# Two transformer blocks on one core: the recurrence's input products in another order, its far decays by biased exponentials, and the queries' norm sums in one piece

## The chip, the cores and the metric

One core of a Trainium2 chip runs the whole program, one launch. The time is device microseconds from the first to the last instruction of that core, with what lies around it; lower is better. The engines are PE (TensorE, matrix products), DVE (VectorE), ACT (ScalarE), POOL (GpSimd) and SP (SyncE, which issues the loads). Each runs its own list of instructions in order and waits at semaphores for the others.

## What is computed

Two blocks, one after the other, on x of 512 tokens by 1024 features, all in float32. The first block is a gated mixer and a feed-forward layer; its mixer has a gMLP branch and a recurrence over 8 heads of width 128:

```python
log_f = jax.nn.log_sigmoid(zf32)            # forget gate
k = jax.nn.sigmoid(-zf32)
q = jax.nn.silu(zq.astype(jnp.float32))
# per chunk of 64 tokens, cum = cumsum(log_f):
o_inter = einsum('bhtk,bhkv->bhtv', qb * exp(cum), state)
scores  = einsum('bhtk,bhsk,bhtsk->bhts', qb, kb, decay)   # decay = exp(cum_t - cum_s), s <= t
state   = state * exp(last) + einsum('bhsk,bhsv->bhkv', kb * exp(last - cum), vb)
# over all chunks, then:
o = rmsnorm(o, norm_g) * jax.nn.silu(heads(zo))
```

The second block is a short convolution mixer with a feed-forward layer, then attention over 16 heads of width 64 with forget gates, whose queries and keys are normalized per head (`rmsnorm_2(q, q_norm)`), and a second feed-forward layer.

## The kernel before, in words

Activations lie with features on the partitions (128 by 512 tokens per tile). Every product is made of three float32r products of high and low halves: `mm3` (L200 to L203) issues xh by wh, xl by wh and xh by wl into one PSUM tile, each 128x512. A product over 1024 inputs (`mm_T`, L205) is eight such triples, and yields after each; `mm_N` (L231) is its form with the tokens on the partitions, four PSUM tiles side by side, 32 yields. Weights are loaded in 1 MB pieces in the order of the list `plan`, and split into halves by ACT (`wh`, L180) and DVE (`wl`, L181), two products ahead of use.

The recurrence of the first block is not run token by token. For each head, `head_in` makes the products zf, zq and zo, and from zf the running sums `sc[:, 1]` (`cum`, sums of log f inside each chunk of 64) and `sc[:, 0]`, the keys `kq[:, 0]` and queries `kq[:, 1]`. `Core.decays(n)` then makes, for level n of 0 to 8, a tile `dec` with the keys and queries scaled for pairs of tokens whose blocks of 2^n tokens are neighbours: for n below 6 POOL subtracts the middle sum twice, and ACT takes the exponential; for n of 6 to 8 the sums are changed in place by DVE (at 7 and 8 two additions of 128x256 each) before one exponential of 128x512. A product by the queries on DVE (POOL at levels 1 and 3) ends each level. `small`, `mid` and `far` are the PE products of levels 0 to 4, 5 to 6 and 7 to 8, all into tiles named `lv`; `values` multiplies by the values (`o`), `square` and `norm` make the sum of squares of the output (`oss`) and its inverse root, and `done` the gated output `y`.

Two generators are woven by `weave`: `main` with the big products of the heads, `side` with the steps of `Core`; `side` starts after HGSTART yields of `main`, and then advances in proportion HGW. A head's `Core` can start only when `head_in` has put it into `heads`; decays of the next head are made up to AHEAD = 4 levels early. `v` is made by `zi_half`, one `mm_N` for four heads each. PE's order follows the weave; the order on ACT, DVE and POOL is set when the program is built, by a scheduler that places what is ready, except for instructions that are pinned (`pin`) to the order of the program.

In the attention stage `HeadNorm` reads a product of queries or keys (`hn`, DVE), squares it (ACT or POOL), splits the square into `hsh` (ACT) and `hsl` (DVE or POOL), sums both over 64 partitions by two products with `bones` on PE (`sums`), and goes on with `hm` (DVE) and `hr` (ACT). `start_norms` issues `sums` for a query after seven of the eight triples of the next product.

Of the kernel before, what the change touches and what calls it, by code (L numbers as in the profile page):

```python
# [8 lines left out]
F32 = mybir.dt.float32  # L9
# [4 lines left out]
ALU = mybir.AluOpType  # L14
# [22 lines left out]
N_FILL = 3  # L37
AHEAD = 4
N_DEC = 8
HGSTART = 36  # L40
HGW = (130, 60)
MUL_POOL = (1, 3)

# [13 lines left out]
def tile_two_blocks(ctx: ExitStack, tc: tile.TileContext, a: dict, out: bass.AP):  # L57
# [137 lines left out]
    def ahead(n):  # L195
        for j in range(state["prep"], n):
            prep(j)
            state["prep"] = j + 1

    def mm3(ps, lh, ll, rh, rl, start, stop_):  # L200
        pe.matmul(ps, lhsT=lh, rhs=rh, start=start, stop=False)  # L201
        pe.matmul(ps, lhsT=lh, rhs=rl, start=False, stop=False)  # L202
        pe.matmul(ps, lhsT=ll, rhs=rh, start=False, stop=stop_)  # L203

# [88 lines left out]
    zf = plan_T("zf", w_in, 0, KD, 2048, 1024)  # L293
    zq = plan_T("zq", w_in, 0, KD, 1024, 1024)
    zo = plan_T("zo", w_in, 0, KD, 4096, 1024)
    for h in range(8):
        if h % 4 == 0:
            plan += plan_N("zi", w_in, 0, KD, 3072 + h * 128)
        plan += [zf[h], zq[h], zo[h]]
    ga = plan_T("ga", w_in, 0, KD, 5120, 1024)  # L300
    ua = plan_T("ua", a["w_up_a"][0], 0, 4, 0, 1024, 512)
    for i in range(8):
# [304 lines left out]
    pool.memset(reset, 1.0)  # L607
    pool.memset(pieces(reset, 64)[:, :, 0:1], 0.0)
    hgs = cp.tile([128, 1], F32, name="hgs")
    ts(dve, hgs, V("hg"), -0.5, ALU.mult)  # L610
    v = [[None, None] for _ in range(NT)]

    def view2(t2, h):
# [4 lines left out]
        return t.rearrange("p (b j i) -> p b j i", j=2, i=h)  # L618

    Y = []  # L620
    heads = {}

    def silu(p, o, g=None):
        t = T("z")
# [15 lines left out]
    def head_in(h):  # L640
        kq, sc = T2("kq"), T2("sc")
        p = yield from mm_T("zf", X)
        t = T("zf")
        tt(dve, t, p, rb)
        e = T("e")
        stt(e, t, -1.0, t, ALU.mult, ALU.min)
        f(e, e, AF.Exp)
        f(e, e, AF.Ln, bias=1.0)
        g = T("g")
        stt(g, t, 0.0, e, ALU.min, ALU.subtract)  # L650
        dve.tensor_tensor_scan(out=sc[:, 1, :], data0=reset, data1=g, initial=0.0, op0=ALU.mult, op1=ALU.add)  # L651
        stt(e, t, 0.0, e, ALU.max, ALU.add)

        tt(pool, sc[:, 0, :], sc[:, 1, :], e, ALU.add)
        f(kq[:, 0, :], e, AF.Exp, scale=-1.0)
        p = yield from mm_T("zq", X)
        silu(p, kq[:, 1, :])
        gate = T("gate")
        p = yield from mm_T("zo", X)
        silu(p, gate, hgs)  # L660
        heads[h] = (kq, sc, gate)

    class Core:


        def __init__(self, h):
            self.h = h
            self.kq, self.sc, self.gate = heads.pop(h)
            self.dec = {}

        def decays(self, n):
            hh = 1 << n
            kq, sc = self.kq, self.sc
            cum = sc[:, 1, :]
            nb = S // (2 * hh)
            e = xp[-1].tile([128, 512], F32, tag="dec", bufs=N_DEC, name=nm("dec"))
            if n < 6:
                c, d = halves(cum, hh), halves(e, hh)
                mid = c[:, :, 0, hh - 1:hh].to_broadcast([128, nb, hh])
                tt(pool, d[:, :, 0, :], mid, halves(sc[:, 0, :], hh)[:, :, 0, :], ALU.subtract)  # L680
                tt(pool, d[:, :, 1, :], c[:, :, 1, :], mid, ALU.subtract)
                f(e, e, AF.Exp)
            else:
                if n == 6:
                    c = pieces(cum, 64)
                    ck = pieces(sc[:, 0, :], 64)
                    tt(dve, ck, c[:, :, 63:64].to_broadcast([128, 8, 64]), ck, ALU.subtract)
                else:
                    h2 = hh // 2
                    sv, pv = halves(sc[:, 0, :], h2), halves(cum, h2)  # L690
                    sh = [128, 2 * nb, h2]
                    tt(dve, sv[:, :, 0, :], sv[:, :, 0, :], pv[:, :, 1, h2 - 1:h2].to_broadcast(sh), ALU.add)
                    tt(dve, pv[:, :, 1, :], pv[:, :, 1, :], pv[:, :, 0, h2 - 1:h2].to_broadcast(sh), ALU.add)
                f(halves(e, hh), view2(sc, hh), AF.Exp)
            eq = halves(e, hh)[:, :, 1, :]
            tt(pool if n in MUL_POOL else dve, eq, eq, halves(kq[:, 1, :], hh)[:, :, 1, :])
            self.dec[n] = e
# [92 lines left out]
        def norm(self):  # L790
            p = PS("oss")
            pe.matmul(p, lhsT=onesr, rhs=self.sq[0], start=True, stop=False)
            pe.matmul(p, lhsT=onesr, rhs=self.sq[1], start=False, stop=True)
            m = T("om")
            ts(dve, m, p, 1.0 / 128, ALU.mult, EPS, ALU.add)
            r = T("or")
            f(r, m, AF.Ln)
            f(r, r, AF.Exp, scale=-0.5)
            gate = self.gate
            tt(pool, gate, gate, r)  # L800
            tt(pool, r, r, r)
            tt(pool, m, m, r)
            self.m = m

        def done(self):
            stt(self.gate, self.m, 3.0, self.gate, ALU.subtract, ALU.mult)
            y = T("y")
            tt(dve, y, self.o, self.gate)
            Y.append(y)
# [58 lines left out]
    M1 = []  # L868

    def main():  # L870
        for h in range(1, 8):
            if h == 4:
                yield from zi_half(1)
            yield from head_in(h)
        rest.extend(split(t) for t in YF)
        for i in range(N_FILL):
            yield from mix_a(i, rest)

# [260 lines left out]
    class HeadNorm:  # L1139
# [14 lines left out]

        def sums(self):
            ps = PS("hn")
            pe.matmul(ps, lhsT=bones, rhs=self.sq[0], start=True, stop=False)
            pe.matmul(ps, lhsT=bones, rhs=self.sq[1], start=False, stop=True)
            self.m = T("hm")
            ts(dve, self.m, ps, 1.0 / 64, ALU.mult, EPS, ALU.add)  # L1160
            r = T("hr")
# [247 lines left out]
```

## Time and profile before

| | us |
|---|---|
| median of 3 runs | 2117.49 |
| lowest and highest | 2116.56, 2117.86 |
| the profiled execution, its own time | 2119.79 |
| span of the trace, first to last instruction | 2118.0 |
| PE busy | 2072.6 (98%) |
| DVE, ACT, POOL busy | 1196.6, 869.8, 476.4 |
| mean granted TensorE clock | 0.988 of full speed |

PE is busy nearly throughout, so time is to be found only where it is not, or where its clock is low. A busy PE row counts a product also when it runs at the lower clock. The recurrence lies at about 75 to 350 us of the span, the keys', queries' and gates' stage at about 1440 to 1700 us.

### The profile page before, as it was taken

What the parts mean: (1) busy time and instruction counts of PE and PEld (TensorE: products, weight loads), DVE (VectorE), ACT (ScalarE), POOL (GpSimd) and SP (SyncE); (2) the same over time, 40 slices, a digit from 0 to 9 for tenths busy, and PEclk for the clock granted to TensorE, in tenths of its full rate; (3) what the DMA queues carried; (4) which work ended last, traced back from release to release, by engine and by line L of the source; (5) the groups of instructions that cost most, each with busy time, mean ns of one, the idle gap of its engine ahead of it and who ended that gap; (6) DMA issues with size and microseconds to landing.
All of it is one profiled execution on the core that took longest, in us unless ns stands there. A gap on an engine that the chain in (4) does not pass through costs nothing.

```text
span 2118.0 us, 27605 instructions
## 1 busy us (share of the span) xinstructions
PE 2072.6 (98%) x11392; PEld 1703.6 (80%) x11392; DVE 1196.6 (56%) x1567; ACT 869.8 (41%) x1347; POOL 476.4 (22%) x423
## 2 busy tenths in 40 slices
PE   8999889999999999999999999999989999999999
PEld 7877767888888888888888888878867778888887
DVE  4698786555443443664555454568566665545453
ACT  5456555543423323422333232345456643323232
POOL 3555654012222222410210010020014311001000
PEclk9999989999999999999999999999989999999999
DMA  6221111323332333233323232232311122323221
GB/s 221 93 68 42 61 61 60 100 100 99 100 99 83 99 98 99 72 107 101 99 85 109 85 112 88 85 115 81 99 41 41 54 67 88 110 80 117 82 90 50
DMA packets 179189, 187.54 MB, mean 89 GB/s; under 512 B 4379, under 2 KB 169976, under 8 KB 179064
## 3 DMA queue, kind: packets, MB, share of 16 engines
q1 hardware_dynamic: 179048, 185.79, 27.1%
q8 instruction: 89, 1.46, 0.3%
q14 instruction: 36, 0.29, 0.0%
q10 hardware_dynamic: 16, 0.00, 0.0%
HBM read 183.68 MB, written 2.10 MB: 88 GB/s over the span
## 4 chain that ended last, share of the span: by engine, by line
PE 88%; DVE 7%; POOL 2%; ACT 2%; issue 1%; DMA 0%; SPq 0%; POOLq 0%; DVEq 0%; ACTq 0%
PE mm L201 26%; PE mm L202 26%; PE mm L203 25%; POOL dec L106 2%; PE mn L242 1%; PE mn L243 1%; PE mn L241 1%; DVE dec L106 1%; DVE sc L106 1%; PE sc L1270 1%; DVE wl L181 1%; PE ao L1319 1%; ACT e L119 1%; PE pt L1306 1%; PE ml L228 1%
## 5 line engine op out<-in xcount | busy, mean ns | idle before, releaser
L201 PE MATMUL mm<-xh,wh 128*128 128x512 f32 x2552 | 1003.8, 394 | 2.2 <-ACT xh L477 2.2
L202 PE MATMUL mm<-xl,wh 128*128 128x512 f32 x2552 | 997.9, 391 | 2.3 <-DVE xl L106 2.3
L203 PE MATMUL mm<-xh,wl 128*128 128x512 f32 x2552 | 997.5, 391 | 0.0
L180 ACT CAST wh<-raw 128x1024 fp32r<-128x1024 f32 (+2 forms) x355 | 364.1, 1026 | 804.1 <-PE mm L202 716.4
L181 DVE TENSOR_TENSOR wl<-raw,wh 128x1024 fp32r<-128x1024 f32 (+2 forms) x355 | 466.8, 1315 | 187.6 <-ACT wh L180 184.0
L201 PEld LDWEIGHTS mm<-xh,wh 128*128 128x128 f32 x2552 | 480.3, 188 | 104.6 <-ACT xh L477 2.4
L202 PEld LDWEIGHTS mm<-xl,wh 128*128 128x128 f32 x2552 | 480.5, 188 | 102.7 <-DVE xl L106 2.8
L203 PEld LDWEIGHTS mm<-xh,wl 128*128 128x128 f32 x2552 | 480.5, 188 | 101.9 <-issue 0.3
L106 POOL TENSOR_TENSOR ua<-ua,rb 128x512 f32<-128x512 f32 x44 | 57.3, 1301 | 592.6 <-ACT ua L119 592.6
L106 DVE TENSOR_TENSOR x<-mm,x 128x512 f32<-128x512 f32 x64 | 44.2, 691 | 154.8 <-PE mm L203 154.8
L106 POOL TENSOR_TENSOR dec<-sc 128x256 f32<-128x256 f32 x96 | 85.1, 917 | 31.6 <-DVE sc L651 23.4
L106 POOL TENSOR_TENSOR acc<-acc,sq 128x512 f32<-128x512 f32 x42 | 66.8, 1591 | 105.6 <-ACT sq L119 83.0
L106 DVE TENSOR_TENSOR a<-mm,rb 128x512 f32<-128x512 f32 x44 | 30.4, 690 | 103.8 <-PE mm L203 103.8
L106 POOL TENSOR_TENSOR rl<-rl 128x512 f32<-128x512 f32 x32 | 48.9, 1529 | 129.4 <-ACT rl L119 129.4
L106 DVE TENSOR_TENSOR sg<-mm,ua 128x512 f32<-128x512 f32 x44 | 30.4, 690 | 83.9 <-POOL ua L106 81.4
L113 POOL TENSOR_SCALAR pe<-pe,rs 128x128 f32<-128x128 f32 (+1 forms) x32 | 30.5, 964 | 183.1 <-DVE rs L1297 175.6
L109 DVE SCALAR_TENSOR_TENSOR ua<-a,convs,ua 128x511 f32<-128x511 f32 x88 | 65.8, 748 | 4.8 <-ACT ua L119 3.3
L241 PE MATMUL mn<-wh,xh 128*128 128x512 f32 x160 | 63.4, 403 | 1.5 <-DVE om L115 1.5
L119 ACT ACTIVATE ua<-ua 128x512 f32<-128x512 f32 x44 | 27.8, 632 | 87.2 <-DVE ua L109 87.2
L242 PE MATMUL mn<-wl,xh 128*128 128x512 f32 x160 | 62.7, 392 | 0.0
L243 PE MATMUL mn<-wh,xl 128*128 128x512 f32 x160 | 60.8, 390 | 0.0
L109 DVE SCALAR_TENSOR_TENSOR xl<-x,vecs,xh 128x512 fp32r<-128x512 f32 x40 | 55.8, 1399 | 5.0 <-ACT xh L119 4.8
(262 smaller groups left out, 1853.5 us busy)
## 6 DMA issues: line engine op xcount, KB each, us to landing
raw<-in_ffn_w_up_dram SPq DMA_DIRECT2D x44, 1024.0 KB
raw<-in_w_ff_dram SPq DMA_DIRECT2D x32, 1024.0 KB
raw<-in_w_in_dram SPq DMA_DIRECT2D x26, 1024.0 KB
raw<-in_ffn_w_down_dram SPq DMA_DIRECT2D x18, 1024.0 KB
raw<-in_a_w_in_dram SPq DMA_DIRECT2D x12, 1024.0 KB
raw<-in_w_kvf_dram SPq DMA_DIRECT2D x8, 1024.0 KB
raw<-in_b_w_qg_dram SPq DMA_DIRECT2D x8, 1024.0 KB
raw<-in_w_up_b_dram SPq DMA_DIRECT2D x4, 1024.0 KB
```

The costliest lines, as they stand in the source:

```text
L106: e.tensor_tensor(out=o, in0=i0, in1=i1, op=op)
L109: dve.scalar_tensor_tensor(out=o, in0=i0, scalar=s, in1=i1, op0=op0, op1=op1)
L113: e.tensor_scalar(out=o, in0=i, scalar1=s1, scalar2=None, op0=op0)
L119: act.activation(out=o, in_=i, func=func, scale=scale, bias=bias, **kw)
L180: act.copy(hi, src)
L181: ins = dve.tensor_tensor(out=lo, in0=src, in1=hi.bitcast(F32), op=ALU.subtract)
L201: pe.matmul(ps, lhsT=lh, rhs=rh, start=start, stop=False)
L202: pe.matmul(ps, lhsT=lh, rhs=rl, start=False, stop=False)
L203: pe.matmul(ps, lhsT=ll, rhs=rh, start=False, stop=stop_)
L241: pe.matmul(pss[j], lhsT=xh[:, t0], rhs=wh[:, kk, :], start=(k + kk == 0), stop=False)
L242: pe.matmul(pss[j], lhsT=xh[:, t0], rhs=wl[:, kk, :], start=False, stop=False)
L243: pe.matmul(pss[j], lhsT=xl[:, t0], rhs=wh[:, kk, :], start=False, stop=(k + kk == nk - 1))
```

## The change

`main` makes both halves of the values first: `zi_half(1)` moves from ahead of head 4 to the start, and HGSTART goes from 36 to 44. zo's product leaves `head_in` and becomes `gate_in`, which runs one head later; the list of weights follows. In `head_in` the minimum of -t and t on DVE becomes an absolute value on ACT. In `decays`, levels 7 and 8 no longer change the sums: the blocks next to the boundary take one exponential of the sums as they are, the others take exponentials of 64 columns each with the missing sums as a per-partition bias (`cum(b)`, and `s2`, `s3`, which two additions of 128x2 make). In `norm`, ACT takes Ln straight from PSUM with scale and bias, POOL multiplies r by r into `om`, and DVE forms the rest in one operation; POOL has one operation fewer. In `HeadNorm.sums` both products are pinned, and so are the first products of the next eight triples. The lines of the changed file are 6 to 39 higher in the rows below.

```diff
-HGSTART = 36
+HGSTART = 44
...
+    behind = [0]
+
     def mm3(ps, lh, ll, rh, rl, start, stop_):
-        pe.matmul(ps, lhsT=lh, rhs=rh, start=start, stop=False)
+        ins = pe.matmul(ps, lhsT=lh, rhs=rh, start=start, stop=False)
+        if behind[0]:
+            pin(ins)
+            behind[0] -= 1
...
-    for h in range(8):
-        if h % 4 == 0:
-            plan += plan_N("zi", w_in, 0, KD, 3072 + h * 128)
-        plan += [zf[h], zq[h], zo[h]]
+    plan += plan_N("zi", w_in, 0, KD, 3072) + [zf[0], zq[0]] + plan_N("zi", w_in, 0, KD, 3584)
+    for h in range(1, 8):
+        plan += [zf[h], zq[h], zo[h - 1]]
+    plan += [zo[7]]
...
-    ts(dve, hgs, V("hg"), -0.5, ALU.mult)
+    ts(dve, hgs, V("hg"), -0.5 / 128, ALU.mult)
+    epsc = cp.tile([128, 1], F32, name="epsc")
+    pool.memset(epsc, EPS)
...
         e = T("e")
-        stt(e, t, -1.0, t, ALU.mult, ALU.min)
-        f(e, e, AF.Exp)
+        f(e, t, AF.Abs)
+        f(e, e, AF.Exp, scale=-1.0)
         f(e, e, AF.Ln, bias=1.0)
...
         silu(p, kq[:, 1, :])
+        heads[h] = (kq, sc)
+
+    def gate_in(h):
         gate = T("gate")
         p = yield from mm_T("zo", X)
         silu(p, gate, hgs)
-        heads[h] = (kq, sc, gate)
+        gates[h] = gate
...
+            def near(t2, k0, q0, nb):
+                base = t2[:, 0, 0:1]
+                return bass.AP(base.tensor, base.offset + k0,
+                               [list(base.ap[0]), [256, nb], [S + q0 - k0, 2], [1, 64]])
+
+            def part(o, j, b, bias):
+                bs = slice(b * 64, b * 64 + 64)
+                f(o[:, bs], sc[:, j, bs], AF.Exp, bias=bias)
...
+                    f(halves(e, hh), view2(sc, hh), AF.Exp)
+                elif n == 7:
+                    ev = e.rearrange("p (b i) -> p b i", i=256)
+                    f(ev[:, :, 64:192].rearrange("p b (j i) -> p b j i", i=64), near(sc, 64, 128, 2), AF.Exp)
+                    for b in (0, 4):
+                        part(e, 0, b, self.cum(b + 1))
+                        part(e, 1, b + 3, self.cum(b + 2))
                 else:
-                    h2 = hh // 2
-                    sv, pv = halves(sc[:, 0, :], h2), halves(cum, h2)
-                    sh = [128, 2 * nb, h2]
-                    tt(dve, sv[:, :, 0, :], sv[:, :, 0, :], pv[:, :, 1, h2 - 1:h2].to_broadcast(sh), ALU.add)
-                    tt(dve, pv[:, :, 1, :], pv[:, :, 1, :], pv[:, :, 0, h2 - 1:h2].to_broadcast(sh), ALU.add)
-                f(halves(e, hh), view2(sc, hh), AF.Exp)
+                    f(e[:, 192:320].rearrange("p (b j i) -> p b j i", b=1, i=64), near(sc, 192, 256, 1), AF.Exp)
+                    s2, s3 = SM("s2")[:, :2], SM("s3")[:, :2]
+                    c = pieces(cum, 64)[:, :, 63]
+                    tt(dve, s2, c[:, 2:5:2], c[:, 3:6:2], ALU.add)
+                    tt(dve, s3, s2, c[:, 1:7:5], ALU.add)
+                    part(e, 0, 2, self.cum(3))
+                    part(e, 1, 5, self.cum(4))
+                    for j in range(2):
+                        part(e, j, 1 + 5 * j, s2[:, j:j + 1])
+                        part(e, j, 7 * j, s3[:, j:j + 1])
...
-            m = T("om")
-            ts(dve, m, p, 1.0 / 128, ALU.mult, EPS, ALU.add)
             r = T("or")
-            f(r, m, AF.Ln)
+            f(r, p, AF.Ln, scale=1.0 / 128, bias=epsc)
             f(r, r, AF.Exp, scale=-0.5)
-            gate = self.gate
+            self.gate = gate = gates.pop(self.h)
+            m = T("om")
+            tt(pool, m, r, r)
+            stt(m, p, 128 * EPS, m, ALU.add, ALU.mult)
             tt(pool, gate, gate, r)
-            tt(pool, r, r, r)
-            tt(pool, m, m, r)
...
-            stt(self.gate, self.m, 3.0, self.gate, ALU.subtract, ALU.mult)
+            stt(self.gate, self.m, 384.0, self.gate, ALU.subtract, ALU.mult)
...
     def main():
+        yield from zi_half(1)
         for h in range(1, 8):
-            if h == 4:
-                yield from zi_half(1)
             yield from head_in(h)
+            yield from gate_in(h - 1)
         rest.extend(split(t) for t in YF)
+        yield from gate_in(7)
...
-            pe.matmul(ps, lhsT=bones, rhs=self.sq[0], start=True, stop=False)
-            pe.matmul(ps, lhsT=bones, rhs=self.sq[1], start=False, stop=True)
+            pin(pe.matmul(ps, lhsT=bones, rhs=self.sq[0], start=True, stop=False))
+            pin(pe.matmul(ps, lhsT=bones, rhs=self.sq[1], start=False, stop=True))
+            behind[0] = 8
```

Three places show how the instructions move. The first is PE at the first query's sums (`hn`), between the products of the second query and the third; before:

```order
L203 MATMUL mm_11951<-xh_11776,wl_11873 128x512
L1157 MATMUL hn_11973<-hsh_11943,bones 128x512
L201 MATMUL mm_12001<-xh_11595,wh_11910 128x512
L202 MATMUL mm_12001<-xl_11596,wh_11910 128x512
L203 MATMUL mm_12001<-xh_11595,wl_11911 128x512
...
L202 MATMUL mm_12001<-xl_11604,wh_11910 128x512
L1158 MATMUL hn_11973<-hsl_11944,bones 128x512
```

and of the change:

```order
L209 MATMUL mm_12025<-xh_11846,wl_11947 128x512
L1195 MATMUL hn_12047<-hsh_12017,bones 128x512
L1196 MATMUL hn_12047<-hsl_12018,bones 128x512
L204 MATMUL mm_12025<-xh_11850,wh_11946 128x512
L208 MATMUL mm_12025<-xl_11851,wh_11946 128x512
L209 MATMUL mm_12025<-xh_11850,wl_11947 128x512
L204 MATMUL mm_12075<-xh_11669,wh_11984 128x512
```

The first half stood after the whole second product, the second half eight products into the third; now both stand ahead of the second product's last triple. For the second and third query the second halves stood 22 and 21 products behind the first.

The second is DVE between head 5's queries and the additions of its far levels (`sc<-sc` 128x4x64 and 128x2x128), before:

```order
L106 TENSOR_TENSOR dec_2900<-dec_2900,kq_2413 128x4x64
L106 TENSOR_TENSOR sc_2414<-sc_2414 128x4x64
L109 SCALAR_TENSOR_TENSOR gate_2695<-z_2737,hgs,sg_2744 128x512
L106 TENSOR_TENSOR sc_2414<-sc_2414 128x4x64
L109 SCALAR_TENSOR_TENSOR gate_1653<-om_2677,gate_1653 128x512
L106 TENSOR_TENSOR y_2760<-o_2590,gate_1653 128x512
L106 TENSOR_TENSOR dec_2904<-dec_2904,kq_2413 128x2x128
L106 TENSOR_TENSOR sc_2414<-sc_2414 128x2x128
```

and of the change, from the queries' z on:

```order
L106 TENSOR_TENSOR z_2663<-mm_2623,rb_510 128x512
L113 TENSOR_SCALAR zc_2665<-z_2663 128x512
L106 TENSOR_TENSOR sc_2398<-sc_2398 128x512
L106 TENSOR_TENSOR kq_2397<-z_2663,sg_2670 128x512
L106 TENSOR_TENSOR dec_2768<-dec_2768,kq_2397 128x256
...
L106 TENSOR_TENSOR dec_2947<-dec_2947,kq_2397 128x4x64
L106 TENSOR_TENSOR z_2735<-mm_2680,rb_510 128x512
L106 TENSOR_TENSOR dec_2951<-dec_2951,kq_2397 128x2x128
```

The four additions are gone, and in this head the in-place subtraction of level 6 (`sc<-sc` 128x512) stands ahead of the queries `kq`; before it stood right behind them.

The third is ACT at the end of head 5's far level, of the change (before, one `dec<-sc` of 128x512 stood there for each of the levels 7 and 8):

```order
L119 ACTIVATE sg_2742<-e_2739 128x512
L119 ACTIVATE dec_2958<-sc_2398 128x128
L119 ACTIVATE dec_2958<-sc_2398 128x64 x2
L119 ACTIVATE dec_2958<-sc_2398,s_484_2960 128x64
L119 ACTIVATE dec_2958<-sc_2398,s_485_2961 128x64
L793 COPY l_463_2761<-lv_2758 128x256
L800 COPY l_465_2766<-lv_2763 128x512
L119 ACTIVATE e_2808<-zf_2806 128x512
```

Seven exponentials (two of the rows repeat and are left out) stand ahead of the copies l of the head before and of the next head's absolute value.

## Rows read from the trace of the kernel before

**Rows 1.** The page, part 4: the chain that ended last, by engine.
```profile
PE 88%; DVE 7%; POOL 2%; ACT 2%; issue 1%; DMA 0%; SPq 0%; POOLq 0%; DVEq 0%; ACTq 0%
```
**Rows 2.** Stretches: us, busy of PE, PEld, DVE, ACT, POOL (count), PEclk, DMA.
```profile
100.00:150.00 50.00, 46.33 (x594) 38.01 (x594) 44.64 (x60) 26.86 (x46) 29.87 (x31) 0.97 0.20 65
150.00:200.00 50.00, 45.98 (x451) 36.56 (x450) 42.51 (x64) 31.67 (x57) 30.89 (x31) 1.00 0.20 64
200.00:250.00 50.00, 47.92 (x642) 39.94 (x641) 39.14 (x60) 28.21 (x51) 25.36 (x25) 0.97 0.20 65
250.00:300.00 50.00, 36.85 (x546) 30.13 (x545) 38.30 (x51) 28.45 (x51) 35.56 (x36) 0.87 0.20 65
300.00:350.00 50.00, 45.19 (x428) 37.09 (x427) 41.87 (x67) 28.91 (x55) 22.20 (x22) 0.86 0.07 22
1500.00:1550.00 50.00, 47.02 (x202) 38.47 (x201) 30.27 (x40) 24.39 (x35) 0.00 (x0) 0.96 0.25 78
1550.00:1600.00 50.00, 47.02 (x297) 35.12 (x296) 33.38 (x67) 29.07 (x74) 11.63 (x13) 0.87 0.09 30
```
**Rows 3.** PE's waits over the span: us in total, times, longest us.
```profile
PE lv L715 <- POOL dec L106: 9.4, 6, 3.3
PE hn L1157 <- ACT hsh L1152: 6.0, 2, 3.0
PE lv L707 <- DVE kq L106: 4.1, 2, 2.8
PE lv L715 <- issue: 3.7, 2, 1.9
PE lv L715 <- DVE dec L106: 2.8, 2, 1.8
```
**Rows 4.** DVE's groups, 75 to 350 us: count, busy us, mean ns, idle before.
```profile
L106 DVE TENSOR_TENSOR sc<-sc 128x256 f32<-128x256 f32 x32 | 24.0, 751 | 0.2
L109 DVE SCALAR_TENSOR_TENSOR e<-zf 128x512 f32<-128x512 f32 x8 | 7.2, 901 | 0.2
L115 DVE TENSOR_SCALAR om<-oss 128x512 f32<-128x512 f32 x7 | 4.8, 682 | 2.0 <-PE oss L793 2.0
L109 DVE SCALAR_TENSOR_TENSOR gate<-om,gate 128x512 f32<-128x512 f32 x6 | 4.6, 772 | 0.0
```
**Rows 5.** ACT's groups, 75 to 350 us, and the timeline at 1562 us.
```profile
L119 ACT ACTIVATE dec<-sc 128x512 f32<-128x512 f32 x24 | 15.1, 629 | 38.4 <-DVE sc L106 38.4
L745 ACT COPY sd<-lv 32x128 f32<-32x128 f32 x16 | 4.0, 250 | 2.0 <-PE lv L741 1.9
L756 ACT COPY l<-lv 128x256 f32<-128x256 f32 x8 | 2.8, 352 | 0.0
1562.05 0.36 ACT L119 ACTIVATE pe<-sc,nmx 128x128 f32<-128x128 f32 x1
```
**Rows 6.** POOL's groups, 75 to 350 us.
```profile
L106 POOL TENSOR_TENSOR om<-om,or 128x512 f32<-128x512 f32 x6 | 8.0, 1340 | 0.5
```
**Rows 7.** Timelines of DVE and POOL, head 5: start, us, instruction, idle before.
```profile
243.27 0.68 DVE L106 TENSOR_TENSOR zf<-mm,rb 128x512 f32<-128x512 f32 x1
251.02 8.86 POOL L106 TENSOR_TENSOR dec<-sc 128x256 f32<-128x256 f32 x11
258.27 1.13 DVE L106 TENSOR_TENSOR kq<-z,sg 128x512 f32<-128x512 f32 x1 [5.13 <-ACT sg L119]
276.71 0.68 DVE L106 TENSOR_TENSOR zf<-mm,rb 128x512 f32<-128x512 f32 x1
```
**Rows 8.** Timelines of DVE and PE, third and fourth query; a 128x2 operation.
```profile
1555.66 0.69 DVE L115 TENSOR_SCALAR hm<-hn 128x512 f32<-128x512 f32 x1 [5.40 <-PE hn L1158]
1556.27 0.68 DVE L106 TENSOR_TENSOR hn<-mm,rb 128x512 f32<-128x512 f32 x1
1559.30 0.49 PE L1157 MATMUL hn<-hsh,bones 128*128 128x512 f32 x1 [2.98 <-ACT hsh L1152]
1565.48 0.16 DVE L1297 RECIPROCAL rs<-sum 128x2 f32<-128x2 f32 x1
```

More of the change, by code (lines that the diff above doesn't have):

```diff
@@ L620, in tile_two_blocks @@
     Y = []
-    heads = {}
+    heads, gates = {}, {}
     def silu(p, o, g=None):
@@ L667, in __init__, with cum @@
             self.h = h
-            self.kq, self.sc, self.gate = heads.pop(h)
+            self.kq, self.sc = heads.pop(h)
             self.dec = {}
+        def cum(self, b):
+            return self.sc[:, 1, b * 64 + 63:b * 64 + 64]
         def decays(self, n):
@@ L793, in norm @@
             pe.matmul(p, lhsT=onesr, rhs=self.sq[1], start=False, stop=True)
+            r = T("or")
+            f(r, p, AF.Ln, scale=1.0 / 128, bias=epsc)
+            f(r, r, AF.Exp, scale=-0.5)
+            self.gate = gate = gates.pop(self.h)
             m = T("om")
-            ts(dve, m, p, 1.0 / 128, ALU.mult, EPS, ALU.add)
-            r = T("or")
-            f(r, m, AF.Ln)
-            f(r, r, AF.Exp, scale=-0.5)
-            gate = self.gate
+            tt(pool, m, r, r)
+            stt(m, p, 128 * EPS, m, ALU.add, ALU.mult)
             tt(pool, gate, gate, r)
-            tt(pool, r, r, r)
-            tt(pool, m, m, r)
             self.m = m
         def done(self):
-            stt(self.gate, self.m, 3.0, self.gate, ALU.subtract, ALU.mult)
+            stt(self.gate, self.m, 384.0, self.gate, ALU.subtract, ALU.mult)
             y = T("y")
```

## The prediction, on record before the result

> **What bounds the kernel now.** I read the chain of waits first: 88% of the path that ended last is PE, 7% DVE, and ACT and POOL 2% each [rows 1]. No product is removed or added by the change, so only PE's idle time and its low clock can be won. The table by stretches says where they are [rows 2]. In the five stretches from 100 to 350 us PE is busy 222.3 of 250 us, so 27.7 us are idle; its clock of 0.97, 1.00, 0.97, 0.87 and 0.86 costs (0.03 + 0.03 + 0.13 + 0.14) x 50 = 16.5 us more. Together 44.2 us are lost in the recurrence, 12.8 of them before 250 us and 31.5 behind it (18.0 idle, 13.5 clock). In the two stretches from 1500 to 1600 us, the queries, 5.96 us are idle and the clock costs (0.04 + 0.13) x 50 = 8.5 us [rows 2].
>
> Then the waits by what ended them [rows 3]. In the recurrence PE waits for `lv` on POOL's and DVE's scaled keys and queries and on `kq`: the small products of a level come when their operands are not there yet. At the queries two waits of 3 us on `hsh` make up all the idle time. The groups show why the decays are late: over 100 to 350 us DVE is busy 44.64 + 42.51 + 39.14 + 38.30 + 41.87 = 206.5 us [rows 2], and PE without its losses would need 250 - 44.2 = 205.8 us. DVE carries as much as PE, while ACT has 144.1 us and POOL 143.9. Last the timeline of one late head: between the products' reads zf of two neighbours, 33.4 us pass (243.27 to 276.71); in it POOL's 11 subtractions run to 259.9, and DVE's `kq` waited 5.13 us for ACT's `sg` [rows 7]. So the four engines form a loop there, with DVE the fullest.
>
> **DVE's share.** Removed are 32 additions of 128x256, 24.0 us, and eight minima, 7.2 us at 901 ns [rows 4]. In `norm` an operation of 682 ns becomes one of the three-operand kind at 772 ns [rows 4], +0.7 us over eight heads. Added are two additions of 128x2 per head, 16 x 0.16 = 2.6 us by the 128x2 row [rows 8]. Net: 31.2 - 3.3 = 27.9 us less, so 178.6 us, 87% of the 205.8 that PE needs.
>
> **ACT's share.** Eight exponentials of 128x512 for each of the levels 7 and 8 go, -16 x 629 ns = -10.1 us, and eight absolute values of the same form come, +5.0 us [rows 5]. In their place stand per head one exponential of 256 columns, 8 x 352 ns = 2.8 us by the copy of that size, one of 128 columns, 8 x 0.36 = 2.9 us, and ten of 64 columns with a bias per partition. No row shows that form. From below, a copy of 32x128 takes 250 ns; from above, the exponential of 128x128 with `nmx` as its bias takes 362 ns, rounded 0.36 [rows 5]. I take 0.30, halfway, 80 x 0.30 = 24.0 us, bounds 20 and 29. Net +24.6 us: 168.7 of 205.8, 82%. Here is the price of the change: it moves DVE's excess to an engine that has room, but cuts it into pieces. The Trainium skill (ScalarE: Activation LUTs, What ACT_TABLE_LOAD costs) puts an activation with a pointer bias at about 280 ns + 0.833 ns per element, an estimate of 333 ns at 64 columns, 26.7 us for the 80 in place of 24.0; the measured 362 ns at 128 columns is under the 387 that it gives there, so I stay with the rows.
>
> The minimum that becomes an absolute value is worth 7.2 - 5.0 = 2.2 us of work, and more by its place: the sums `sc` come out of that chain. By the rows this operation is shorter on ACT (629 ns) than on DVE (901 ns) [rows 4, 5]. The Trainium skill (ScalarE: Activation LUTs, Rules for kernel authors) says the reverse, that maxima, minima, additions and products belong on VectorE; by it the 7.2 us would stay on DVE as the better bargain, and the sum below would be some 5 us smaller (7.2 of 27.9 us of its 21 us). The measured durations of this kernel speak against it.
>
> **POOL's share.** One of three operations of `norm` goes: 8 x 1.34 = 10.7 us [rows 6], leaving 133.2 us. It stands in front of the next head's subtractions, so this shortens the loop too.
>
> **The order.** zo one head behind takes its reads and its `silu` off the stretch between zq and the small products. A triple takes 3 x 47.02 / 202 = 0.70 us [rows 2]; by the order of instructions heads 4 to 7 have 16 triples more, 11.2 us, between zq and the first small product, and heads 1 to 3 lose the same, since the second half of the values is in front. The weights' list follows the order of use, and the DMA engines are at 0.20 [rows 2], so I cost the loads at nothing; were that cover gone, a late 1 MB piece would show as a wait of PE on `wh`. The gate comes a head later but is only read in `norm`. What is late next: in heads 1 and 5 the subtraction of level 6, which waits for POOL, stands ahead of `kq` on DVE; and the loop of POOL's subtractions, ACT's exponentials, `sg` and `kq` remains, with seven exponentials ahead of the copies `l`.
>
> **What the recurrence gains.** Below, nothing: the loop turns at POOL's and ACT's pace. Above, all 44.2 us less the 3.7 us that PE waited for nothing visible [rows 3], 40.5 us. If DVE kept its present share of the stretch, 206.5 / 250 = 0.826, the 250 us would become 178.6 / 0.826 = 216.2, 33.8 us less. I take less: in 100 to 250 us the lead shrinks while DVE is relieved, so the 12.8 us stay; of the 31.5 us behind 250 two thirds go, **-21 us**.
>
> **What the queries gain.** Both sums now stand ahead of the last triple of the next product, and nothing can be put between them. Now the second half comes 8 to 22 products late; DVE's `hm` waited 5.40 us for it, and the read `hn` of the next query stands behind that wait at 1556.27; so that query's `hsh` is late, and PE waits 2.98 us for it at 1559.30 [rows 8]. With the halves together `hm` starts some 5 us earlier and both waits, 5.96 us, go. The clock falls in the same stretches; I take 5.5 of its 8.5 us, some two thirds, between 0 and 8.5. **-11.5 us** together, bounds -14.5 and +12 (third rival).
>
> Sum: -32.5 us against the profiled execution's 2119.8 gives 2087.3; that execution is 2.3 us above the median of 2117.5, so the forecast is **2085.0 us**, with a range of its own of 2074 to 2098 (a third of the 32.5 us either way).
>
> **The rivals.** First, all comes back: at 0.87 DVE no longer holds the loop, and the clock stays up: -40.5 - 14.5 = -55, so 2062 to 2074. For it speaks that DVE is the fullest engine, against it the 11 subtractions in a row and the shorter lead of heads 1 to 3. Second, the loop of POOL and ACT holds and the recurrence gains only 5 us: -16.5, 2101, or 2098 to 2113. For it speaks that the longest waits end on POOL [rows 3] and that ACT gets 24.6 us more. Third, the pinned pair waits: asked for a triple earlier, PE waits 2.98 + 0.70 + 0.68 = 4.4 us for the low half (0.68 us is an operation of 128x512 on DVE [rows 7]), at four sums 17.4 us instead of 5.96, with no gain of clock: -21 + 11.5, 2108. Against it: the wait is now for a read held up by `hm`, which goes. Fourth, **slower**: ACT becomes the bound. The biased exponentials stand in its queue ahead of `l` and of the next head's absolute value; if ACT's loop of a head exceeds PE's, its 24.6 / 8 = 3.1 us per head lie on the path, 7 x 3.1 = 21.5 us, nothing is gained in the recurrence, and -11.5 at the queries leaves +10: 2127. It decides when ACT is nearly full between two heads; at 82% it is not, unless its waits for DVE's `sc`, 38.4 us now [rows 5], persist. The Trainium skill's rule above, elementwise work to VectorE, would lead here. Fifth, the change does not do what it says: the relieved DVE is not what PE waits for, the shorter lead of heads 1 to 3 costs what the later heads gain, and at the queries another read is late: 2113 to 2122.
>
> **How the numbers follow.** Forecast 0.53, first 0.10, second 0.18, third 0.04, fourth 0.09, fifth 0.06. The range from 2064 to 2112 takes in the forecast, the third and most of the first two; left out are the fourth, the fifth and 0.02 of the first and the second each, 0.19. A measurement tells apart 0.2%, 4.2 us (2113.3 to 2121.7): faster 0.85, the same 0.06, slower 0.09.
>
> **What would show it.** In the changed profile: the group of additions of 128x256 gone, DVE near 180 us and ACT near 169 in those 250 us of work; exponentials of 128x64 near 0.30 us; in the stretches behind 250 us, PE's idle and clock losses of 31.5 us down to about 10, with shorter waits of `lv` on `dec` and `kq`; at the queries no wait on `hsh`, and the clock above 0.95. I am wrong if PE waits longer on `dec` by ACT, on `kq` in the early heads, or on `hsl`; if the 64-column exponentials take 0.36 or more; or if the clock stays low without waits.

## The result, and the profile after

The changed kernel takes 2099.77 us against 2117.02 us before, a ratio of 0.9915 with the interval 0.9898 to 0.9932: 17.3 us faster, where 32.5 were forecast. In five more rounds it took 2098.82 against 2117.38 us, 0.9908 (0.9894 to 0.9921), and the profile of that run is used here, since the first profiled execution ran at a granted clock of 0.751 throughout. Its own time is 2097.71 us, its span 2096.0, 22.0 us shorter than the span before; that is 3.4 us more than between the medians, since the two profiled executions lie 2.4 us above theirs and 1.1 below. No run says in which stage these 3.4 us lie, so what a stage gave, as read from the two profiles, can be that much too large.

The chain of waits of the changed kernel has PE at 90% where it had 88, DVE at 4 where it had 7 [rows 1]:

```profile
PE 90%; DVE 4%; POOL 3%; ACT 2%; issue 1%; DMA 0%; SPq 0%; POOLq 0%; DVEq 0%; ACTq 0%
```

Its table by stretches, with the columns of [rows 2]:

```profile
100.00:150.00 50.00, 48.12 (x614) 39.88 (x613) 36.21 (x52) 31.07 (x66) 23.34 (x25) 1.00 0.27 86
150.00:200.00 50.00, 45.80 (x630) 37.12 (x630) 39.40 (x52) 35.39 (x74) 34.59 (x36) 1.00 0.14 44
200.00:250.00 50.00, 41.59 (x427) 33.73 (x426) 38.33 (x60) 32.74 (x69) 28.01 (x30) 0.97 0.19 64
250.00:300.00 50.00, 45.29 (x598) 37.14 (x598) 41.44 (x66) 35.52 (x81) 28.39 (x31) 0.97 0.26 86
300.00:350.00 50.00, 48.19 (x467) 39.82 (x466) 33.00 (x53) 35.46 (x72) 18.83 (x20) 1.00 0.19 65
...
1500.00:1550.00 50.00, 48.56 (x263) 37.91 (x262) 35.84 (x61) 29.01 (x61) 5.33 (x4) 1.00 0.27 85
1550.00:1600.00 50.00, 49.74 (x396) 38.27 (x395) 33.51 (x66) 31.23 (x82) 21.10 (x20) 1.00 0.13 43
1600.00:1650.00 50.00, 46.76 (x361) 36.11 (x360) 33.41 (x69) 32.77 (x89) 18.60 (x18) 0.93 0.13 43
```

From 100 to 350 us PE is idle for 21.0 us (27.7 before), and the clock costs 0.06 x 50 = 3.0 (16.5 before). The gain there is clock far more than waits. (The stretches are fixed in time, so each holds work that ran some 15 to 25 us later before.) From 1500 to 1600 us 1.7 us of idle time are left of 6.0, at full clock; but from 1600 to 1650, where nothing was lost before, there are now 3.2 us idle and 3.5 us of clock. PE's waits over the span say which (us in total, times, longest):

```profile
PE oss L830 <- POOL osl L106: 11.3, 5, 3.9
PE lv L752 <- issue: 5.1, 3, 1.9
PE pt L1345 <- DVE pe L113: 4.2, 3, 2.6
...
PE lv L752 <- POOL dec L106: 2.2, 2, 1.8
```

Against [rows 3], `hn` on `hsh` is gone, `lv` on `kq` too, and `lv` on POOL's `dec` fell from 9.4 to 2.2. In their place stand `oss` on `osl`, the low half of the squared outputs that `oss` sums (3.6 before), and a wait that was not there: `pt`, the turning of the softmax's shares, on DVE's `pe`.

Where the time came from can be read from one row of DVE, the 16 `hm` of keys and queries: its first start marks the end of the recurrence's effect, its last that of the queries'. (Behind x16: shortest, median and longest in ns, then first and last start.) The kernel before:

```profile
L115 DVE TENSOR_SCALAR hm<-hn x16: 682/688/692, 1450.7 to 1661.0; 128x512 f32<-128x512 f32 x16
```

The changed kernel:

```profile
L115 DVE TENSOR_SCALAR hm<-hn x16: 670/688/692, 1434.1 to 1633.4; 128x512 f32<-128x512 f32 x16
```

The first comes 16.6 us earlier, the last 27.6, the end 22.0. So between these two executions the recurrence gave 16.6 us, keys and queries 11.0 more, and 5.6 of that were given back between the last `hm` and the end.

The groups of the changed kernel, 75 to 350 us, on the three engines (count, busy us, mean ns, idle before):

```profile
L106 DVE TENSOR_TENSOR s<-s,sc 128x2 f32<-128x2 f32 x8 | 9.7, 1210 | 0.2
L109 DVE SCALAR_TENSOR_TENSOR om<-oss,om 128x512 f32<-128x512 f32 x8 | 5.5, 682 | 1.8 <-POOL om L106 1.8
L106 DVE TENSOR_TENSOR s<-sc 128x2 f32<-128x2 f32 x8 | 4.3, 538 | 0.0
L119 ACT ACTIVATE dec<-sc 128x64 f32<-128x64 f32 x48 | 13.4, 335 | 0.0
L119 ACT ACTIVATE dec<-sc,s 128x64 f32<-128x64 f32 x32 | 8.5, 334 | 0.0
L119 ACT ACTIVATE e<-zf 128x512 f32<-128x512 f32 x8 | 5.1, 632 | 6.8 <-DVE zf L106 6.8
L106 POOL TENSOR_TENSOR dec<-sc 128x256 f32<-128x256 f32 x96 | 79.1, 854 | 82.1 <-DVE sc L659 81.6
```

The far exponentials no longer wait for `sc`, where those of 128x512 had an idle time of 38.4 us on `sc` ahead of them [rows 5]. In part ACT now waits elsewhere: its `dec<-dec` exponentials of the small levels waited 11.7 us for POOL and now wait 20.3. The mean and the busy time of the 64-column rows differ: 80 times 0.334 us would be 26.8 us, but ACT is busy with them for 21.9 (13.4 + 8.5), because they overlap.

### The profile page after: what moved, and what is told of

Same layout as the page of the kernel before. It is cut to its first block, busy times and chain, and to the rows that moved or that the text cites. A ratio compares the mean times of both kernels' runs of the same rounds, so it can differ in the third digit from the quotient of the medians.

```text
span 2569.7 us, 27675 instructions
## 1 busy us (share of the span) xinstructions
PE 2549.3 (99%) x11392; PEld 1806.0 (70%) x11392; DVE 1155.3 (45%) x1543; ACT 894.6 (35%) x1435; POOL 469.5 (18%) x416
## 4 chain that ended last, share of the span: by engine, by line
PE 98%; ACT 0%; issue 0%; DMA 0%; DVE 0%; SPq 0%; POOL 0%; DVEq 0%; POOLq 0%
PE mm L204 28%; PE mm L208 28%; PE mm L209 28%; PE mn L249 2%; PE mn L248 2%; PE mn L247 2%; PE o L818 1%; PE ao L1358 1%; PE sc L1309 1%; PE pt L1345 1%; PE ml L234 1%; PE ml L233 1%; PE ml L232 1%; PE lv L752 0%; PE lv L797 0%
## 5 line engine op out<-in xcount | busy, mean ns | idle before, releaser
L204 PE MATMUL mm<-xh,wh 128*128 128x512 f32 x2552 | 1172.8, 460 | 0.1
L209 PE MATMUL mm<-xh,wl 128*128 128x512 f32 x2552 | 1166.6, 458 | 0.0
L208 PE MATMUL mm<-xl,wh 128*128 128x512 f32 x2552 | 1166.5, 457 | 0.0
L204 PEld LDWEIGHTS mm<-xh,wh 128*128 128x128 f32 x2552 | 508.1, 199 | 214.2 <-issue 2.5
L209 PEld LDWEIGHTS mm<-xh,wl 128*128 128x128 f32 x2552 | 508.6, 199 | 213.1 <-issue 1.8
L208 PEld LDWEIGHTS mm<-xl,wh 128*128 128x128 f32 x2552 | 509.2, 200 | 210.9 <-issue 1.8
L181 DVE TENSOR_TENSOR wl<-raw,wh 128x1024 fp32r<-128x1024 f32 (+2 forms) x355 | 442.0, 1245 | 317.7 <-ACT wh L180 297.0
L249 PE MATMUL mn<-wh,xl 128*128 128x512 f32 x160 | 71.5, 458 | 0.0
L106 DVE TENSOR_TENSOR rs<-mm,rb 128x512 f32<-128x512 f32 x32 | 22.1, 689 | 104.7 <-PE mm L209 104.7
L106 POOL TENSOR_TENSOR x<-x,rs 128x512 f32<-128x512 f32 x24 | 44.2, 1843 | 118.8 <-DVE rs L106 118.8
```

Of the source, the lines that this page charges most:

```text
L106: e.tensor_tensor(out=o, in0=i0, in1=i1, op=op)
L181: ins = dve.tensor_tensor(out=lo, in0=src, in1=hi.bitcast(F32), op=ALU.subtract)
L204: ins = pe.matmul(ps, lhsT=lh, rhs=rh, start=start, stop=False)
L249: pe.matmul(pss[j], lhsT=xl[:, t0], rhs=wh[:, kk, :], start=False, stop=(k + kk == nk - 1))
```

## The experiments

Twelve runs; medians of 4 to 11 timings, but for the eleventh, which has one. "The change" in the expectations is the changed kernel. Spans and `hm` rows of single profiles differ by 1 or 2 us for reasons outside the edits (the second run is 1.2 us behind at its first `hm`, ahead of which it does nothing else than the kernel before), so the times are compared by medians.

**The change again (1)** is the run of the section above.

> The changed kernel once more, for a profile at the usual clock (its first profile ran at a granted clock of 0.751 throughout). Both theories: 2099.8 us, 0.9915 of before. Theory A (the loop of POOL and ACT holds the recurrence, the queries gave the larger part): idle time plus clock loss of 100 to 350 us between 25 and 40 us, no wait on hsh in 1500 to 1600 us. Theory B (the recurrence gave nearly all): under 30 us lost from 100 to 350 us, and the waits and low clock of 1500 to 1600 us much as before.

Neither theory as put: idle and clock lost 24.0 us, just under A's band, the queries lost their waits on `hsh`, and the recurrence gave more than the queries.

**The pair alone (2)**: the kernel before with the diff's lines in `mm3` and `sums`.

> The kernel before with the pinned pair of sums alone. Theory A: 11.5 us faster than before, 2105.5 us (0.9946), both waits on hsh gone. Theory B: within 3 us of before. The prediction's third rival (PE waits for the low half): 2 to 12 us slower than before, waits on hsl in place of hsh.

2114.18 us, 0.9981 (0.9972 to 0.9990): 3.2 us faster, not 11.5. Its row, and PE's waits from 1400 to 1750 us:

```profile
L115 DVE TENSOR_SCALAR hm<-hn x16: 669/688/692, 1451.9 to 1652.8; 128x512 f32<-128x512 f32 x16
```

```profile
PE pt L1312 <- DVE pe L113: 4.2, 3, 2.6
PE pt L1312 <- POOL pe L113: 1.4, 2, 0.8
PE pt L1312 <- DVE rs L1303: 0.8, 1, 0.8
```

Between first and last `hm` pass 200.9 us where 210.3 passed: 9.4 us gained. The span is only 3.4 shorter: 1.2 us are lost ahead of the first `hm`, and 4.8 are given back behind the last, where the new waits for `pt` follow. The same rows appear in the changed kernel, so this belongs to the pins and not to the recurrence.

**The pins early only (5)**:

```diff
-            pin(pe.matmul(ps, lhsT=bones, rhs=self.sq[0], start=True, stop=False))
-            pin(pe.matmul(ps, lhsT=bones, rhs=self.sq[1], start=False, stop=True))
-            behind[0] = 8
+            hold = pin if self.by is act else (lambda ins: ins)
+            hold(pe.matmul(ps, lhsT=bones, rhs=self.sq[0], start=True, stop=False))
+            hold(pe.matmul(ps, lhsT=bones, rhs=self.sq[1], start=False, stop=True))
+            behind[0] = 8 if self.by is act else 0
```

> The changed kernel with the pinned sums only for the keys and the first four queries; the last four queries go back to unpinned sums and unpinned products. The second run showed the pin's gain, 10.3 us at the queries, given back by 7.2 us behind them, where PE waits for pt. Theory A (the pin holds the big products back behind the last queries' sums, so that none of them covers the softmax there): the wait for pt of 4.2 us on pe of DVE goes, 2093 to 2095 us, 4 to 6 us faster than the change. Theory B (DVE, ACT and POOL simply have no more to give in that stage, so PE that comes earlier must wait): the wait stays, within 1.5 us of the change.

2095.53 us, 0.9904 (0.9888 to 0.9919). The interval overlaps the change's; the medians differ by 3.3 us, and runs 9 and 10, which differ by the same edit, by 3.7 with no overlap of their times (2103.49 to 2106.04 and 2100.09 to 2102.61). (The expectation's 10.3 and 7.2 us are 9.4 and 4.8 by the rows of run 2.) The `hm` of run 5:

```profile
L115 DVE TENSOR_SCALAR hm<-hn x16: 671/689/692, 1435.2 to 1636.6; 128x512 f32<-128x512 f32 x16
```

From the last `hm` to the end of the span (2093.5 us) pass 456.9 us. In the kernel before it was 457.0, in the changed kernel 462.6. Every run fits this: 456.9 to 457.0 us in the three with early pins (5, 10 and 12), 461.6 to 463.0 in the nine with all pins. So what was given back comes from the late pins, and is gone without them; in exchange the first and last `hm` of run 5 are 201.4 us apart, not 199.3.

The place is behind the last query's sums. PE in the changed kernel (start, us, instruction, idle before):

```profile
1632.70 0.39 PE L1195 MATMUL hn<-hsh,bones 128*128 128x512 f32 x1
1632.93 0.39 PE L1196 MATMUL hn<-hsl,bones 128*128 128x512 f32 x1
...
1635.85 0.66 PE L1345 MATMUL pt<-ident,pe 128*128 128x128 f32 x4
...
1636.93 0.24 PE L1317 MATMUL sc<-steps,picks 64*128 64x64 bf16 x4
1639.73 0.88 PE L1345 MATMUL pt<-ident,pe 128*128 128x128 f32 x3 [2.56 <-DVE pe L113]
1641.08 0.87 PE L1345 MATMUL pt<-ident,pe 128*128 128x128 f32 x3 [0.47 <-DVE rs L1336]
```

and with the pins early only:

```profile
1639.09 0.66 PE L1346 MATMUL pt<-ident,pe 128*128 128x128 f32 x4
1639.50 0.48 PE L204 MATMUL mm<-xh,wh 128*128 128x512 f32 x1
...
1640.42 0.24 PE L1318 MATMUL sc<-steps,picks 64*128 64x64 bf16 x4
1640.59 0.50 PE L208 MATMUL mm<-xl,wh 128*128 128x512 f32 x1
...
1645.07 0.39 PE L209 MATMUL mm<-xh,wl 128*128 128x512 f32 x1
1645.30 0.82 PE L1346 MATMUL pt<-ident,pe 128*128 128x128 f32 x6
```

With the next eight triples pinned to the program's order, the second `pt` comes right behind the scores, and PE sits 2.56 us until DVE has the shares; unpinned, 20 products of 128x512 stand between scores and `pt`, from 1640.59 to 1645.30, and cover it. The wait on DVE's `pe` is gone from this run's list; POOL's 1.4 us stay, and 2.2 us on `xh` come, the wait that stood behind the attention in the kernel before too. The two sums of each late query stand as close together in run 5 as in the changed kernel, though nothing pins them; what has moved is the triples. Theory A by the rows; its time is half a us above that theory's band.

**The order undone (3)**: the old list of weights, HGSTART 36, `zi_half(1)` ahead of head 4, and the gate product back in `head_in`.

> The changed kernel with the old order of products (values' second half ahead of head 4, gate product right behind zq, start after 36 yields). Theory A (the order gives the late heads lead, and takes it from the early ones, so half of the recurrence's gain): 2103 to 2106 us, 3 to 6 us slower than the change. Theory B, the order gives the whole gain of the recurrence: 2108 to 2117. A third, that the shorter lead of the early heads costs what the late ones gain: within 2 us of the change.

2099.90 us, 0.9914 (0.9900 to 0.9927): the third. One wait stands for another: `lv` on `kq` is back with 2.9 us and `lv` on DVE's `dec` with 4.0, while `oss` on `osl` falls to 0.9.

**The far levels undone (4)**: levels 7 and 8 as in the kernel before.

> The changed kernel with the old levels 7 and 8 (two additions of 128x256 on DVE each, one exponential of 128x512), all else as changed. If DVE's load holds the recurrence, 24.0 us back on DVE make it 8 to 15 us slower than the change, 2108 to 2115. If the loop of POOL and ACT holds it (theory A), within 3 us of the change; if the biased exponentials on ACT are a net cost, 3 to 8 us faster, 2092 to 2097.

2104.03 us, 0.9935 (0.9923 to 0.9948): 5.2 us slower, which fits no theory's band. The groups, 75 to 350 us:

```profile
L106 DVE TENSOR_TENSOR sc<-sc 128x256 f32<-128x256 f32 x32 | 16.0, 500 | 0.2
L119 ACT ACTIVATE dec<-sc 128x512 f32<-128x512 f32 x24 | 15.1, 628 | 22.2 <-DVE sc L106 21.5 <-PE lv L740 0.7
```

The 32 additions take 500 ns there on average, not the 751 of [rows 4], because fewer of them run beside POOL (see the last section), and ACT's exponentials of 128x512 wait 21.5 us for `sc`. PE's longest waits there are those for `osl`, 9.7 us; none of its waits is put down to the far exponentials.

**The absolute value (7) and the norm (8) undone**, each by its lines of the diff.

> The changed kernel with the minimum of -t and t back on DVE in place of the absolute value on ACT. If that chain sets when a head's sums are ready, 2 to 4 us slower than the change (8 x 0.27 us plus a place in DVE's row); if not, within 1.5 us. By the rule of the Trainium skill (ScalarE: Activation LUTs, Rules for kernel authors: minima and maxima on VectorE) it would be faster than the change.

> The changed kernel with the old norm (scale and eps by DVE ahead of Ln, three operations on POOL). Far levels gave 6.5 us of the recurrence's 16.3 and the order nothing, so some 10 us are left for the norm and the absolute value. If the norm's shorter row on POOL gives them: 5 to 8 us slower than the change. If the parts only count together: within 2 us.

2099.83 us, 0.9916 (0.9902 to 0.9929), and 2102.51 us, 0.9931 (0.9918 to 0.9943). The absolute value is worth 1.0 us, no more than the two medians of the changed kernel differ by; the norm 3.7 (2101.19 to 2105.18 against 2097.71 to 2099.12). With order 1.1, far levels 5.2 and the pair 3.2 the parts sum to 14.2 of 18.6 us. Four of these were measured by taking a part away and the pair by putting it in alone, and two are within the noise, so the 4.4 us that are left are not assigned: that the parts help each other is possible, and not shown.

**The low half on DVE (6)**:

```diff
-            tt(pool, self.sq[1], sq, self.sq[0].bitcast(F32), ALU.subtract)
+            tt(dve, self.sq[1], sq, self.sq[0].bitcast(F32), ALU.subtract)
```

> The changed kernel with osl, the low half of the squared outputs, on DVE instead of POOL. PE waits 11.3 us for it in the changed kernel, where it stands behind seven or more subtractions in POOL's row. Theory A (the row on POOL is the recurrence's new wait): the waits of oss on osl fall below 3 us and the kernel is 5 to 9 us faster than the change, 2090 to 2094. Theory B (DVE is still what bounds the loop; 8 x 0.7 us more on it): the wait moves to lv on dec or kq, and the time stays within 2 us of the change.

2099.91 us, 0.9917 (0.9904 to 0.9931): the same. The 11.3 us became 3.1 on DVE's `osl`, 3.4 on ACT's `osh`, and a lower clock (0.90 from 250 to 300 us). Theory B in the time, though not at the rows that it named.

**Fewer pieces on ACT (9, 10)**: level 8's far blocks get their missing sums from level 7's in-place additions.

```diff
+                    sv, pv = halves(sc[:, 0, :], 64), halves(cum, 64)
+                    sh = [128, 3, 64]
+                    tt(dve, sv[:, 0:3, 0, :], sv[:, 0:3, 0, :], pv[:, 0:3, 1, 63:64].to_broadcast(sh), ALU.add)
+                    tt(dve, pv[:, 1:4, 1, :], pv[:, 1:4, 1, :], pv[:, 1:4, 0, 63:64].to_broadcast(sh), ALU.add)
+                    f(halves(e, hh), view2(sc, hh), AF.Exp)
...
+                    f(e[:, 0:128], sc[:, 0, 0:128], AF.Exp, bias=sc[:, 1, 255:256])
+                    f(e[:, 384:512], sc[:, 1, 384:512], AF.Exp, bias=sc[:, 1, 383:384])
```

> The changed kernel with level 7 by two in-place additions again, of 128x192 instead of 128x256, and one exponential of 128x512; level 8 by one exponential of 256 columns and two of 128 columns whose bias is one of the sums, so without s2 and s3. In the changed kernel's profile s2 and s3 take 0.54 and 1.21 us where 0.16 each was taken, and the ten exponentials of 64 columns 0.334 each. Per head this gives ACT 4.05 - (0.62 + 0.41 + 2 x 0.39) = 2.2 us back at the same work on DVE (1.2 in place of 1.75 us). Theory A (ACT's pieces are what is left of the loop): 4 to 8 us faster than the change, 2091 to 2095. Theory B (the loop is POOL's subtractions and the latency of the chain): within 2 us.

> The last one with the sums pinned for the keys and the first four queries alone. The two parts lie in different stages and should add: 3.3 us faster than the run without it, whatever that gives; by theory A 2087 to 2092 us, by theory B 2094 to 2096.

2104.70 us, 0.9938 (0.9925 to 0.9950), and 2101.05 us, 0.9921 (0.9907 to 0.9934): 5.9 us slower than the change and 5.5 slower than run 5, with less work on both engines. Run 9's groups, and PE's longest wait, 75 to 400 us:

```profile
L106 DVE TENSOR_TENSOR sc<-sc 128x192 f32<-128x192 f32 x16 | 7.2, 449 | 0.1
L119 ACT ACTIVATE dec<-sc 128x512 f32<-128x512 f32 x16 | 10.1, 629 | 14.5 <-DVE sc L106 14.3
L119 ACT ACTIVATE dec<-sc 128x128 f32<-128x128 f32 x16 | 5.5, 390 | 0.0
```

```profile
PE oss L817 <- POOL osl L106: 12.5, 4, 4.5
```

DVE has 7.2 us of additions in place of 14.0, ACT 18.9 us (10.1 + 5.5 + 3.3 for the 256 columns) for the two far levels and level 6 in place of 32.6 (5.0 + 13.4 + 8.5 + 3.3 + 2.4). So neither engine's load is what the biased exponentials paid for. What came back with the additions is the chain, addition behind exponential behind addition: 14.3 us of ACT's waiting for `sc`. PE's idle time from 100 to 350 us is even (20.4 us against 21.0); the clock is not, 0.97, 0.97, 0.97, 0.90 and 1.00, 9.5 us against 3.0. Runs 4 and 9 both bring the chain back and are both slower, with hardly more or even less work on DVE; that speaks for the chain as the cost. It isn't shown by itself, since with each edit the scheduler places the other instructions anew, and how the chain lets PE's clock fall stays open.

**The sums apart (11)**, one timing: `s3` from two of the sums instead of `s2` and a sum.

> The changed kernel with s3 made without s2, from the sums alone; one of the three sums is left out of each far bias. It measures the 128x2 additions. If the second takes 1.21 us because it reads what the one ahead has just written, it falls to 0.57 us like the first; if it is the reading of two far columns that takes long, it stays near 1.2. The time: within 3 us of the change.

The second addition then takes 0.15 us in every head, and 1.19 to 1.23 us where it reads `s2`. DVE in the changed kernel and in this run, which groups the two:

```profile
210.75 0.57 DVE L106 TENSOR_TENSOR s<-sc 128x2 f32<-128x2 f32 x1
211.36 1.22 DVE L106 TENSOR_TENSOR s<-s,sc 128x2 f32<-128x2 f32 x1
```

```profile
211.09 0.64 DVE L106 TENSOR_TENSOR s<-sc 128x2 f32<-128x2 f32 x2
```

So it is the dependence on what the first addition has just written; in six heads that one stands right ahead, in two another DVE instruction stands between, and the second takes 1.21 us there too. The first takes 0.44 to 0.57 us in both kernels. The time, 2098.72 us, doesn't move though 8.5 us of these additions went: once more DVE's load is not the bound.

**The norm later (12)**: run 5 with `norm` behind `far`.

```diff
             yield 800
-            if h:
-                cores[h - 1].norm()
-                yield 500
             c.far()
             look(9 * h + 9 + AHEAD)
-            yield 2000
+            yield 1500
             if h:
+                cores[h - 1].norm()
+                yield 1000
                 cores.pop(h - 1).done()
```

> The changed kernel with the sums pinned early alone (run 5) and the norm of the head before placed behind the far products instead of between the middle and the far ones, so that PE comes to oss some 15 products later. In all runs with the changed order PE waits 8 to 12 us for osl, and putting osl on DVE took the wait away but no time. Theory A (that wait is lost time because PE has nothing else in front of it; the products that now stand ahead cover it): the waits of oss fall below 2 us, 5 to 8 us faster than run 5, 2088 to 2091. Theory B (POOL and ACT turn the loop of a head, PE waits elsewhere for the same time): lv waits on dec in place of oss, within 2 us of run 5.

2103.87 us, 0.9937 (0.9923 to 0.9950): 8.3 us slower than run 5. PE's waits, 75 to 400 us:

```profile
PE lv L752 <- POOL dec L106: 16.9, 5, 6.3
PE lv L752 <- issue: 4.0, 2, 2.1
```

The wait for `osl` is gone and stands at `lv` on `dec`, longer. The place is that of theory B; the time is neither theory's. Here as in run 6, taking one wait out of a head's loop let PE wait at another.

## Why the prediction was right or wrong

The time lies in the range, 12 us inside its upper end, but 1.8 us outside the likeliest case's own range. Direction and stages were right, and the gain was put nearly twice too high; the range held because it took in most of the second rival's too. Of the 32.5 us forecast, the two profiled executions show 22.0: 4.4 are missing in the recurrence, 0.5 at the queries, and 5.6 came back behind them. The medians show 3.4 us less still.

**The queries** were sized well: -11.5 forecast, -11.0 between the rows of `hm` (-9.4 in run 2); both waits went, for the reason given ([rows 8]: `hm` behind the late second half). The step that failed here is the sum, which took this stage's gain for the end's. 5.6 us came back, at `pt`. The working costed the pin of the two sums and never that of the next eight triples, whose freedom covered the softmax's latency; its list of what is late next named the recurrence alone. The third rival looked for a wait at the pair itself, and there was none. That nothing can be put between the two sums was not so: in the changed kernel's trace 10 to 17 other products stand between the halves of three of the 16 pairs (a key's, the fourth and the fifth query's).

**The recurrence** was put at -21; it gave 16.6. By the forecast's own measure, idle time plus clock, it went from 44.2 to 24.0, 20.2 us, so the mis-sized step is the one from this measure to time. The measure counts in part twice: a stretch's low clock was charged for all its 50 us, also for those in which PE stood idle. Charged for PE's busy time alone, the clock costs 14.0 and 2.6 us and not 16.5 and 3.0, which explains 2.2 of the 3.6 us; the rest is open. The late part came down as forecast (31.5 to about 10; 8.0 measured). The early part, taken to stay at 12.8, is 16.0, of which 9.9 lie from 200 to 250 us, where `oss` waits 6.6 us for `osl`.

**The engines.** POOL is 133.2, forecast and measured, but by some luck: eight operations of 1.34 us were taken off, of which the stretch held six [rows 6], and the 96 subtractions, of which the forecast says nothing, take 79.1 us where they took 85.1. ACT is 170.2 (168.7). A 64-column exponential lasts 0.334 us where 0.30 was taken, and the Trainium skill's estimate of 333 ns (ScalarE: Activation LUTs, What ACT_TABLE_LOAD costs) agrees with these rows. As load neither fits, since the 80 overlap: 21.9 us, where the forecast took 24.0 and the estimate gave 26.7. What ACT has more than forecast is work that now falls into the stretch, as 32 large casts `wh` where there were 30, and eight heads' `norm` where there were seven. DVE is 188.4, not 178.6: the additions of 128x2 cost 14.0 us, not 2.6, which is more than the whole difference. The row of 0.16 us [rows 8] was one of an operation whose input, the `sum` that ACT made, DVE had not just written. Nor were the 24.0 us of [rows 4] what the additions cost by themselves: 14 of the 32 ran beside POOL, and at the 0.42 us of the others they come to 13.4 us. The same holds for the minimum's 901 ns, which are 690 in the four heads where POOL did nothing meanwhile, so the row spoke less clearly for ACT than it seemed.

**The reason** for the gain was wrong in part. The prediction saw DVE's load. Runs 9 and 11 lighten DVE and gain nothing; what the runs point to is that the far exponentials read sums which nobody changes. The 38.4 us in [rows 5] stood there as this chain's price, and the prediction used them only as a condition of its fourth rival. The Trainium skill's rule that puts minima on VectorE was weighed against the durations; run 7 shows neither side's gain, its 1.0 us being within the noise.

**The rivals.** The second, at 2101, came nearest in time, but by luck and not by its mechanism: the recurrence gained 16.6 us, not 5. A loop is nevertheless what is left: in runs 6 and 12 the waits change their place and idle time plus clock loss does not fall, 27.7 us in run 6 and 40.0 in run 12 against 24.0 in the changed kernel and 25.8 in run 5. The fourth did not happen; ACT, at 170.2 of the 205.8 us (83%), is not full.

**Open** is which of the loop's links sets its length. POOL's 96 subtractions, 79.1 us of work in rows of up to eleven, were changed in no run; nor was the changed kernel run with all pins taken out. The fastest version is run 5, by its median 3.3 us ahead of the change.

## What to carry to other kernels

When a wait is removed by fixing an order, ask what the freedom that is lost had covered further on; here pins that helped at the first queries cost half of the gain at the last. Where work is moved off an engine, check whether its load or its place in a chain was the price: try a version with less load and the same chain. Idle time and the low clock of a stretch can overlap, so charge the clock for the busy time alone before the two are added.

## What the runs showed of the hardware

The second of two DVE additions of 128x2 took 1.19 to 1.23 us in all eight heads where it reads what the first has just written, and 0.15 us where it does not (run 11). The first took 0.44 to 0.57 us in both; the runs don't say why.

In-place additions of 128x256 on DVE, at the same shapes, took 0.41 to 0.43 us where POOL did little or nothing meanwhile (18 of the 32 before) and 0.78 to 1.51 us, 1.18 on average, where POOL worked for over half of their time (14 of 32). In run 4 only four of them ran beside POOL, and the mean fell from 751 to 500 ns. Four additions of one head of the kernel before, with POOL's row at that time (POOL is idle from 234.44 to 242.65 us; the first two are grouped, 1.49 and 0.42 us):

```profile
233.11 1.33 POOL L106 TENSOR_TENSOR om<-om,or 128x512 f32<-128x512 f32 x1
233.24 1.95 DVE L106 TENSOR_TENSOR sc<-sc 128x256 f32<-128x256 f32 x2
236.22 0.42 DVE L106 TENSOR_TENSOR sc<-sc 128x256 f32<-128x256 f32 x1
237.16 0.42 DVE L106 TENSOR_TENSOR sc<-sc 128x256 f32<-128x256 f32 x1
```

So a mean duration of a DVE row can hold time that goes with POOL's work, and it need not stay when the order changes.
